# An MLP in split float32 on one Trainium2 core: when its first and last operands are formed, and when x1 is copied out

## The chip, the core and the metric

The kernel runs on one core of a Trainium2 chip. The core has five engines that work side by side and wait for each other by semaphores: TensorE (PE in the profile; PEld is its weight load), VectorE (DVE), ScalarE (ACT), GpSimd (POOL) and SyncE (SP), whose queue issues nearly all DMAs here. The metric is the device time of one execution in microseconds (us), the median of three runs. The kernel before takes 1250.95 us (1249.01 to 1251.21).

## What is computed

One decoder layer for a prompt of 1024 tokens and a sample group of 8 x 8 tokens: a mixing part (retention, window attention, two convolutions, an output projection) and then an MLP, all in float32. The change lies in the MLP, so the reference is cut to that:

```python
x = x + gate1[:, None] * mixed
h2 = rms_norm(x, norm2_g[l]) * (1.0 + scale2[:, None]) + shift2[:, None]
ff = jnp.square(jax.nn.relu(h2 @ w_ff1[l])) @ w_ff2[l]     # 1024 -> 4096 -> 1024
x = x + gate2[:, None] * ff
```

## The kernel before

Everything is held feature by feature on the 128 partitions, tokens along the free axis. `x1` (128 x 8 x 1088) is x after the first residual: 1024 prompt columns and 64 sample columns. Float32 products are made of two parts: an operand is cast to fp32r on ACT (`ah`, `qh`, `wh`: the high part), DVE subtracts that from the original (`al`, `ql`, `wl`: the low part), and a product is three matmuls, high by high, high by low, low by high. `two` (line 1260) makes both parts at once; `form` (line 1386) makes the cast and hands back the subtraction, to be placed later. A 128 x 1024 cast and the subtraction behind it are the unit of work that this text speaks of.

**First product (ff1).** The 4096 hidden features are 32 blocks of 128 rows, four blocks to a group, so 8 groups. A block is computed in three chunks of columns (384, 384 and 320, the last with the sample's 64). A chunk of a block is 24 matmuls (`ff1_block`), and ACT then applies Relu and Square into the group's tiles (`ff1_out`). `Group.quarter(i, j)` is rows 2i and 2i+1 of the group's four blocks, prompt columns 512j to 512j+511; each quarter is a tile of 128 x 1024 (`q11`, `q12`, `q21`, `q22`).

**Second product (ff2).** Group g's 512 hidden rows times w_ff2's 512 x 1024 is a 2 x 2 by 2 x 2 product of quarters. For groups 0 to 6 it is done with seven quarter products in place of eight (Strassen's scheme in Winograd's form): sums of weight quarters (`s`) and of activation quarters (`t`) are formed on DVE, split in two parts, and each of the seven `slot`s is four PE products of six matmuls each, whose results DVE adds to `x1`. Between the slots the 12 ff1 chunks of the next group are spread (`ff1_items`; f counts them, block f // 3, chunk f % 3). The sample's columns go through PE apart: `sample_parts` makes the tile `st` (a cast and a subtraction), `sample_product` multiplies it with weight parts into the bank `sm`, `sample_out` adds the result to `acc`. The last group, 7, is done with plain products, sixteen PE products of twelve matmuls each (i, t and m in line 1579 on), and closes the residual: `x1 * gate + xr + ps * gate`, where `xr` is x1 as it was before the MLP. Since DVE adds the products into `x1` itself, x1 is copied to DRAM first (`save`, line 1377) and read back in 8 pieces (line 1562).

**Order.** PE's instructions keep the order of the program throughout. ACT's and DVE's do from line 1378 on (`pinned`); ahead of it a scheduler places them. SP's DMA issues are placed by the scheduler. Each engine's queue is served in order: an instruction that waits holds up all behind it. Buffers come from pools by tag; `w`, `ar`, `wh`, `wl`, `ah`, `al`, `qh`, `ql` and `q12` have two each, `fr`, `t` and the other quarters one. A new tile of a tag waits until the readers of the tile before the last are done. `w` and `ar` take the weight quarters from DRAM, `fr` the ff1 weights of the blocks from 4 on. PE's results go round seven PSUM banks (`next_bank`).

The places of the change. (1) Ahead of the loop: blocks 0 to 3 of ff1 chunk by chunk, then the split of block 4's weights, then `first_parts` (line 1431): the sum `t`, and both parts of weight quarter (0,0) and activation quarter (0,0), which slot 1 multiplies. (2) The same `first_parts` at the end of each group (line 1544), behind slot 7 and the sample products and ahead of the last ff1 chunk, f = 11. (3) The end of the last loop turn and the sixteen plain products (lines 1547 to 1595), where all of the last group's operands are split one after another.

Of the kernel before, what the change touches and what calls it, by code (L numbers as in the profile page):

```python
# [15 lines left out]
P = 128  # L16
# [124 lines left out]
def decoder_step(ctx: ExitStack, tc: tile.TileContext, A, O, where):  # L141
# [1042 lines left out]
    with ExitStack() as fctx:  # L1184
# [54 lines left out]
        def make_h2(c):  # L1239
            c0, w = CH[c]  # L1240
            h2[c] = act_chunk(c)
            r = room("t")[:, :w]
            ps = misc_psum()[:, :w]
            average(ps, ones_r, ssq_parts[c])
            rstd(ps, w, r, ut(w))
            b = mod[:, 24:32, :]
            for k in range(8):
                modulated(h2, c, k, x1[:, k, c0 : c0 + w], r, a2, b, ut(w))
            if c == 2:
                t = sums[:, 0:512].rearrange("p (k n) -> p k n", k=8)  # L1250
                DVE.tensor_tensor(out=t, in0=x1[:, :, SEQ:], in1=r[:, PROMPT[2] :].unsqueeze(1).to_broadcast([P, 8, 64]),
                                  op=ALU.mult)
                modulated_sample(h2, t, a2, b)
# [6 lines left out]
        def two(raw, hi_tag, lo_tag):  # L1260
            hi, lo = room(hi_tag, F32R), room(lo_tag, F32R)
            cast(raw, hi, lo)()
            return hi, lo
# [33 lines left out]
        def quarter(g, i, j):  # L1297

            raw = room(RAW[turn["raw"] % 4])
            turn["raw"] += 1  # L1300
            nc.sync.dma_start(raw.rearrange("p (q f) -> p q f", q=2),
                              A["w_ff2"][g, 2 * i : 2 * i + 2].rearrange("q p f -> p q f")[:, :, H * j : H * j + H])
            return raw
# [42 lines left out]
        def ff1_load(x, tag="fr"):  # L1346
            if x < NG * G:
                ff1_weights[x] = loaded_weight(A["w_ff1"][x], room(tag))

        def ff1_split(x, hi="wh", lo="wl"):  # L1350
            if x < NG * G:
                ff1_weights[x] = two(ff1_weights[x], hi, lo)
# [4 lines left out]
        def ff1_out(u, x, c, ps):  # L1357
            for cols, dst in u.pieces(x % G, c):
                ACT.activation(dst, ps[:, cols], AF.Relu)
                ACT.activation(dst, dst, AF.Square)  # L1360


        for b in range(G):
            ff1_load(b, "w" if b < 2 else "ar")
            ff1_split(b, *(("wh", "wl") if b < 2 else ("ah", "al")))
        u = Group()
        for c in range(3):
            for b in range(G):
                ps = mm_psum(CH[c][1])
                ff1_block(u, b, c, ps)  # L1370
                if c == 0 and b == 1:
                    make_h2(2)
                ff1_out(u, b, c, ps)
        ff1_load(G)

        save = nc.dram_tensor("x1_save", (P, 8, SEQ), F32, kind="Internal").ap()
        nc.sync.dma_start(save, x1[:, :, 0:SEQ])
        pinned[0] = True
        acc = wide_room("acc")
        BANKS = [f"mm{x}" for x in range(4)] + [f"pm{x}" for x in range(3)]  # L1380
# [5 lines left out]
        def form(raw, side):  # L1386

            parts = room(side + "h", F32R), room(side + "l", F32R)
            return parts, cast(raw, *parts)
# [13 lines left out]
        def sample_parts(g, u):  # L1403

            st = up.tile([P, G, P], F32R, tag="st", name=nm("st"), bufs=1)
            ACT.copy(st[:, :, 0:64], u.sample)
            DVE.tensor_tensor(out=st[:, :, 64:P], in0=u.sample, in1=st[:, :, 0:64], op=ALU.subtract)
            return st
# [16 lines left out]
            return pp.tile([P, 512], F32, tag="pm3", name=nm("sm"))  # L1425

        sub, add = ALU.subtract, ALU.add
        ff1_split(G)
        ff1_load(G + 1)

        def first_parts(g, u, a11):

            t = room("t")
            DVE.tensor_tensor(out=t, in0=u.quarter(0, 1), in1=u.quarter(0, 0), op=sub)
            w, r0 = form(a11, "a")
            v, r1 = form(u.quarter(0, 0), "q")
            r0()
            r1()
            return t, (w, v)

        a11 = quarter(0, 0, 0)
        t, now_parts = first_parts(0, u, a11)
        s = quarter(0, 1, 0)
        a22, a12 = quarter(0, 1, 1), quarter(0, 0, 1)

        for g in range(NG - 1):
            nu = Group()
# [2 lines left out]
            def ff1_items(n):  # L1450
                for _ in range(n):
                    f = state["f"]
                    state["f"] += 1
                    b, c = f // 3, f % 3
                    x = G * (g + 1) + b
                    ps = next_bank()[:, : CH[c][1]]
                    ff1_block(nu, x, c, ps)
                    ff1_out(nu, x, c, ps)
                    if c == 0:
                        ff1_split(x + 1)  # L1460
                        ff1_load(x + 2)
# [68 lines left out]
            slot(parts6, [(1, 1, 0, 0), (0, 1, 1, 0)], [r0, r1])  # L1530
            last = g + 1 == NG - 1
            s = quarter(g + 1, 0 if last else 1, 1 if last else 0)
            ff1_items(2)


            w, r0 = form(a21, "a")
# [4 lines left out]
            sample_out(g, 1, sm)  # L1541
            if not last:
                a11 = nxt
                t, now_parts = first_parts(g + 1, nu, a11)
                a22, a12 = quarter(g + 1, 1, 1), quarter(g + 1, 0, 1)
            else:
                weights, parts = {(0, 0): two(nxt, "ah", "al")}, {(0, 0): two(nu.quarter(0, 0), "qh", "ql")}
            ff1_items(1)
            u = nu


        g = NG - 1
        weights[0, 1] = two(s, "ah", "al")
        for ij, tags in (((1, 0), ("qh", "ql")), ((0, 1), ("q12", "t")), ((1, 1), ("fr", "q11"))):
            parts[ij] = two(u.quarter(*ij), *tags)
        st = sample_parts(g, u)
        for j in range(2):
            weights[1, j] = two(quarter(g, 1, j), "wh", "wl")
        xr = [hp.tile([P, 4, CH[0][1]], F32, tag=("hi0", "lo0", "hi1", "lo1")[m % 4], name=nm("xr")) for m in range(8)]
        xr = [x.rearrange("p a b -> p (a b)")[:, 0:SEQ] for x in xr]  # L1560
        for m in range(8):
            nc.sync.dma_start(xr[m], save[:, m, :])
        s22 = x1[:, 4:8, H:SEQ]
        for x in (x1[:, 0:4, H:SEQ], x1[:, 4:8, 0:H]):
            DVE.tensor_tensor(out=x, in0=x, in1=s22, op=ALU.add)

        def sample_end(i):

# [8 lines left out]
            nc.sync.dma_start(O["yT"][:, 4 * i : 4 * i + 4, SEQ:], x)  # L1577

        for i in range(2):
            sm = sample_bank()  # L1580
            for j in range(2):
                sample_product(sm, st, weights[i, j], j, j == 0, j == 1)
            sample_out(g, i, sm)
            for t in range(2):
                for m in range(4):
                    ps = next_bank()
                    for j in range(2):
                        products(ps, m, weights[i, j], parts[j, t], j == 0, j == 1)
                    x = x1[:, 4 * i + m, H * t : H * t + H]
                    gate = mod[:, 40 + 4 * i + m, 0:1]  # L1590
                    DVE.scalar_tensor_tensor(x, x, gate, xr[4 * i + m][:, H * t : H * t + H], ALU.mult, ALU.add)
                    DVE.scalar_tensor_tensor(x, ps, gate, x, ALU.mult, ALU.add)
                    if t == 0 and m == 1:
                        sample_end(i)
                    nc.sync.dma_start(O["yT"][:, 4 * i + m, H * t : H * t + H], x)


# [72 lines left out]
```

## Time and profile before

| | |
|---|---|
| median of three runs | 1250.95 us (1249.01 to 1251.21) |
| the profiled execution, its own time | 1249.56 us |
| its span, first to last instruction | 1247.8 us |
| mean granted TensorE clock | 0.992 of full |
| PE busy | 1215.0 us (97% of the span) |
| DVE busy | 819.2 us (66%) |
| ACT busy | 469.8 us (38%) |
| DMA, HBM read and written | 101.90 MB and 10.72 MB |

The profile is one execution, taken by the hardware profiler. A line such as `ps<-qh,ah` names the tile written and the tiles read, by the program's names. Engines overlap, so shares add up to more than 100%. A matmul is shown from its start to its modelled end, and the next one starts before that end: 128 x 512 matmuls follow each other every 0.23 us though each is shown with 0.39 us. A bracket at the end of a line of the timeline, such as `[0.44 <-DVE ql L158]`, is the time for which the engine stood idle ahead of it and what ended that. Line 158 is the helper that records ACT's and DVE's instructions and line 171 the one that records PE's, so places are told apart by tile names.

### The profile page before, as it was taken

How to read it: one execution, taken by the hardware profiler on the slowest of the kernel's cores; microseconds unless marked ns; L12 is line 12 of the kernel's file. 1: busy time of each engine (PE TensorE's matmuls, PEld its weight loads, DVE VectorE, ACT ScalarE, POOL GpSimd, SP SyncE). 2: the span in 40 equal slices, each digit the busy share in tenths (PEclk: the TensorE clock that was granted, in tenths of full speed). 3: DMA queues.
4: the chain of work that ended last, by engine and by line, in shares of the span. 5: the costliest groups of instructions: out<-in, count | busy, mean ns of one | idle time of the engine just before them, and what ended most of it. 6: DMA issues, size and time to landing. Idle time of an engine off the chain costs nothing.

```text
span 1247.8 us, 17276 instructions
## 1 busy us (share of the span) xinstructions
PE 1215.0 (97%) x7044; PEld 1099.9 (88%) x7044; DVE 819.2 (66%) x1297; ACT 469.8 (38%) x943; POOL 30.0 (2%) x43
## 2 busy tenths in 40 slices
PE   8899999999999999989999999999999999999978
PEld 6797789998899999979989989989989989989967
DVE  4779798884797538546466666566475575575574
ACT  5362333342366315533333334333333333333320
POOL 3300000000000000000000000000000000000000
PEclk9899999999999999989999999999999999999989
DMA  9548811111020811311211221221121221211512
GB/s 364 180 142 306 231 52 51 50 38 35 35 71 22 279 47 34 136 34 51 74 62 68 68 56 64 68 83 53 56 79 51 68 68 51 85 51 51 185 55 89
DMA packets 54982, 113.73 MB, mean 91 GB/s; under 512 B 13431, under 2 KB 22391, under 8 KB 54903
## 3 DMA queue, kind: packets, MB, share of 16 engines
q1 hardware_dynamic: 54759, 112.56, 27.6%
q8 instruction: 55, 0.90, 0.3%
q14 instruction: 24, 0.20, 0.1%
q10 hardware_dynamic: 144, 0.07, 0.0%
HBM read 101.90 MB, written 10.72 MB: 90 GB/s over the span
## 4 chain that ended last, share of the span: by engine, by line
PE 87%; DVE 9%; DMA 2%; ACT 1%; issue 1%; SPq 0%; DVEq 0%
PE ps L171 48%; PE mm L171 29%; PE pm L171 5%; PE sm L171 3%; DVE x L158 1%; PE pm L175 1%; PE ada L171 1%; DVE al L158 1%; DVE ql L158 1%; DMA ada<-in_ada 1%; DMA M<-in_xT 1%; DMA glu<-in_st_conf 0%; ACT ah L158 0%; DVE qh L301 0%; DVE lo L308 0%
## 5 line engine op out<-in xcount | busy, mean ns | idle before, releaser
L171 PE MATMUL ps<-hi,wl 128*128 128x384 f32 (+1 forms) x672 | 219.4, 326 | 0.0
L171 PE MATMUL ps<-hi,wh 128*128 128x384 f32 (+1 forms) x672 | 219.2, 326 | 0.0
L171 PE MATMUL ps<-lo,wh 128*128 128x384 f32 (+1 forms) x672 | 219.0, 326 | 0.0
L171 PE MATMUL mm<-hi,wh 128*128 128x384 f32 (+1 forms) x536 | 178.4, 333 | 0.1
L171 PE MATMUL mm<-lo,wh 128*128 128x384 f32 (+1 forms) x536 | 174.8, 326 | 2.0 <-DVE lo L476 2.0
L171 PE MATMUL mm<-hi,wl 128*128 128x384 f32 (+1 forms) x536 | 174.4, 326 | 0.5 <-DVE wl L252 0.5
L158 ACT ACTIVATE q<-ps 128x384 f32<-128x384 f32 (+1 forms) x112 | 42.6, 381 | 350.9 <-PE ps L171 350.9
L158 DVE TENSOR_TENSOR x<-x,ps 128x512 f32<-128x512 f32 x264 | 165.9, 682 | 1.0
L171 PE MATMUL ps<-ql,ah 128*128 128x512 f32 x408 | 160.9, 394 | 4.4 <-DVE ql L158 4.4
L171 PE MATMUL ps<-qh,ah 128*128 128x512 f32 x408 | 159.9, 392 | 3.9 <-ACT qh L158 3.9
L171 PE MATMUL ps<-qh,al 128*128 128x512 f32 x408 | 160.0, 392 | 0.0
L171 PEld LDWEIGHTS ps<-hi,wh 128*128 128x128 f32 x672 | 126.2, 188 | 2.2
L171 PEld LDWEIGHTS ps<-lo,wh 128*128 128x128 f32 x672 | 126.1, 188 | 2.2
L171 PEld LDWEIGHTS ps<-hi,wl 128*128 128x128 f32 x672 | 126.1, 188 | 0.0
L158 DVE TENSOR_TENSOR wl<-fr,wh 128x1024 fp32r<-128x1024 f32 x28 | 34.3, 1225 | 134.4 <-ACT wh L158 134.4
L171 PEld LDWEIGHTS mm<-hi,wh 128*128 128x128 f32 x536 | 100.6, 188 | 7.7 <-issue 6.0
L171 PEld LDWEIGHTS mm<-lo,wh 128*128 128x128 f32 x536 | 100.7, 188 | 2.9 <-DVE lo L476 2.9
L171 PEld LDWEIGHTS mm<-hi,wl 128*128 128x128 f32 x536 | 100.6, 188 | 0.8 <-DVE wl L252 0.8
L609 DVE SCALAR_TENSOR_TENSOR M<-glu,cmix,M 128x512 f32<-128x512 f32 (+2 forms) x150 | 98.1, 670 | 2.0
L171 PEld LDWEIGHTS ps<-ql,ah 128*128 128x128 f32 x408 | 77.0, 189 | 22.1 <-DVE ql L158 7.1
L171 PEld LDWEIGHTS ps<-qh,ah 128*128 128x128 f32 x408 | 77.2, 189 | 19.0 <-ACT qh L158 4.2
L171 PEld LDWEIGHTS ps<-qh,al 128*128 128x128 f32 x408 | 77.0, 189 | 16.0
(340 smaller groups left out, 1876.9 us busy)
## 6 DMA issues: line engine op xcount, KB each, us to landing
w<-in_w_ff SPq DMA_DIRECT2D x29, 512.0 KB, 3.6
ar<-in_w_ff SPq DMA_DIRECT2D x28, 512.0 KB, 3.7
fr<-in_w_ff SPq DMA_DIRECT2D x28, 512.0 KB, 3.6
w<-in_w_in SPq DMA_DIRECT2D x22, 512.0 KB, 5.1
M<-in_ada SPq DMA_DIRECT2D x20, 512.0 KB, 4.7
ada<-in_ada SPq DMA_DIRECT2D x16, 512.0 KB, 10.4
sw<-in_ada SPq DMA_DIRECT2D x9, 512.0 KB, 5.2
w<-in_w_out SPq DMA_DIRECT2D x8, 512.0 KB, 3.6
```

The source lines that it names most:

```text
L158: i = f(*args, **kw)
L171: return tc.keep_in_program_order(nc.tensor.matmul(*args, **kw))
L175: return tc.keep_in_program_order(nc.tensor.transpose(*args, **kw))
L609: DVE.scalar_tensor_tensor(dst, src(t), cdw[:, j, t : t + 1], dst, ALU.mult, ALU.add))))
```

## The change

Seven edits.

- The last chunk of the first four blocks (c = 2) is computed in the block order 2, 3, 0, 1.
- Ahead of it the four weight quarters of group 0 are requested, and behind them x1's copy to DRAM, now in three pieces by columns. Block 4's weights are requested earlier, in chunk 0.
- The parts of slot 1's operands in group 0 are made by `two` in the buffers `ah`, `al`, `qh`, `ql` within the last chunk, and `t` behind it (`first_sum`).
- In each group one ff1 chunk, f = 10, moves from ahead of slot 7 to behind it, and the parts of the next slot 1 are made ahead of both remaining chunks, with `t` behind the parts.
- In the last loop turn the same place makes the parts of (0,0), then of weight quarter (0,1) in `wh`, `wl`, ahead of f = 10, and those of activation quarter (1,0) between f = 10 and f = 11.
- The sixteen plain products start at once. The parts of the remaining activation quarters and of the sample are made behind the first of them, the remaining weight quarters' behind the third and fourth, the sample's products come behind the fourth, its end behind the sixth.
- The two wide additions of `s22` to x1 are taken apart, one behind the first product and one ahead of the eighth's closing.

```diff
         u = Group()
+        save = nc.dram_tensor("x1_save", (P, 8, SEQ), F32, kind="Internal").ap()
         for c in range(3):
-            for b in range(G):
+            for b in range(G) if c < 2 else (2, 3, 0, 1):
                 ps = mm_psum(CH[c][1])
                 ff1_block(u, b, c, ps)
                 if c == 0 and b == 1:
                     make_h2(2)
+                    ff1_load(G)
                 ff1_out(u, b, c, ps)
-        ff1_load(G)
-
-        save = nc.dram_tensor("x1_save", (P, 8, SEQ), F32, kind="Internal").ap()
-        nc.sync.dma_start(save, x1[:, :, 0:SEQ])
+                if c == 1 and b == 3:
+                    a11 = quarter(0, 0, 0)
+                    s, a22, a12 = (quarter(0, *ij) for ij in ((1, 0), (1, 1), (0, 1)))
+                    for c0, w in zip((0, 384, 768), PROMPT):
+                        nc.sync.dma_start(save[:, :, c0 : c0 + w], x1[:, :, c0 : c0 + w])
+                if c == 2 and b == 3:
+                    now_parts = two(a11, "ah", "al"), two(u.quarter(0, 0), "qh", "ql")
+        ff1_split(G)
+        ff1_load(G + 1)
...
-        def first_parts(g, u, a11):
+        def first_sum(u):
             t = room("t")
             DVE.tensor_tensor(out=t, in0=u.quarter(0, 1), in1=u.quarter(0, 0), op=sub)
-            w, r0 = form(a11, "a")
-            v, r1 = form(u.quarter(0, 0), "q")
-            r0()
-            r1()
-            return t, (w, v)
+            return t
...
             slot(parts6, [(1, 1, 0, 0), (0, 1, 1, 0)], [r0, r1])
             last = g + 1 == NG - 1
             s = quarter(g + 1, 0 if last else 1, 1 if last else 0)
-            ff1_items(2)
+            ff1_items(1)
...
             if not last:
                 a11 = nxt
-                t, now_parts = first_parts(g + 1, nu, a11)
+                now_parts = two(a11, "ah", "al"), two(nu.quarter(0, 0), "qh", "ql")
+                t = first_sum(nu)
                 a22, a12 = quarter(g + 1, 1, 1), quarter(g + 1, 0, 1)
+                ff1_items(2)
             else:
                 weights, parts = {(0, 0): two(nxt, "ah", "al")}, {(0, 0): two(nu.quarter(0, 0), "qh", "ql")}
-            ff1_items(1)
+                weights[0, 1] = two(s, "wh", "wl")
+                ff1_items(1)
+                parts[1, 0] = two(nu.quarter(1, 0), "q12", "t")
+                ff1_items(1)
             u = nu
 
         g = NG - 1
-        weights[0, 1] = two(s, "ah", "al")
-        for ij, tags in (((1, 0), ("qh", "ql")), ((0, 1), ("q12", "t")), ((1, 1), ("fr", "q11"))):
-            parts[ij] = two(u.quarter(*ij), *tags)
-        st = sample_parts(g, u)
-        for j in range(2):
-            weights[1, j] = two(quarter(g, 1, j), "wh", "wl")
+        raw = [quarter(g, 1, j) for j in range(2)]
...
         for i in range(2):
-            sm = sample_bank()
-            for j in range(2):
-                sample_product(sm, st, weights[i, j], j, j == 0, j == 1)
-            sample_out(g, i, sm)
             for t in range(2):
                 for m in range(4):
                     ps = next_bank()
                     for j in range(2):
                         products(ps, m, weights[i, j], parts[j, t], j == 0, j == 1)
+                    if i == t == m == 0:
+                        parts[0, 1] = two(u.quarter(0, 1), "qh", "ql")
+                        parts[1, 1] = two(u.quarter(1, 1), "fr", "q11")
+                        st = sample_parts(g, u)
+                    if (t, m) == (i, 0) and i == 0 or (t, m) == (1, 3) and i == 0:
+                        x = x1[:, 0:4, H:SEQ] if m == 0 else x1[:, 4:8, 0:H]
+                        DVE.tensor_tensor(out=x, in0=x, in1=s22, op=ALU.add)
...
+                    if i == 0 and t == 0 and m >= 2:
+                        weights[1, m - 2] = two(raw[m - 2], "ah", "al") if m == 3 else two(raw[0], "wh", "wl")
+                    if t == 0 and m == 3:
+                        sm = sample_bank()
+                        for j in range(2):
+                            sample_product(sm, st, weights[i, j], j, j == 0, j == 1)
+                        sample_out(g, i, sm)
+                    if t == 1 and m == 1:
+                        sample_end(i)
```

What this does to the queues is shown at three places. First DVE, at the start of the MLP's second product; before:

```order
L158 TENSOR_TENSOR wl_5311<-fr_5306,wh_5310 128x1024
L158 TENSOR_TENSOR t_5318<-q_721_5096,q_700_4929 128x1024
L158 TENSOR_TENSOR al_5321<-w_5316,ah_5320 128x1024
L158 TENSOR_TENSOR ql_5324<-q_700_4929,qh_5323 128x1024
L158 TENSOR_TENSOR w_5328<-w_5328,ar_5330 128x1024
L158 TENSOR_TENSOR al_5336<-w_5328,ah_5335 128x1024
```

and after, where `ql_5266`, `al_5262` are the low parts of slot 1's operands, `wl_5328` that of block 4's weights, `t` the activations' sum, `w_5193` the weights' sum `s` and `al_5338` its low part:

```order
L1258 TENSOR_TENSOR ql_5266<-q_700_4929,qh_5265 128x1024
L1258 TENSOR_TENSOR al_5262<-w_5191,ah_5261 128x1024
L1258 TENSOR_TENSOR wl_5328<-fr_5014,wh_5327 128x1024
L158 TENSOR_TENSOR t_5334<-q_722_5098,q_700_4929 128x1024
L158 TENSOR_TENSOR w_5193<-w_5193,ar_5195 128x1024
L158 TENSOR_TENSOR al_5338<-w_5193,ah_5337 128x1024
```

The three low parts that stood behind or around `t` stand ahead of it; `t`, `s` and the part of `s` follow as before.

Second DVE at the end of a group (the first), behind the four additions of slot 7; before:

```order
L158 TENSOR_TENSOR acc_5309<-sm_6703,acc_5309 128x512
L158 TENSOR_TENSOR t_6713<-q_859_6157,q_853_6118 128x1024
L158 TENSOR_TENSOR al_6716<-ar_6498,ah_6715 128x1024
L158 TENSOR_TENSOR ql_6719<-q_853_6118,qh_6718 128x1024
L158 TENSOR_TENSOR ar_6603<-ar_6603,w_6723 128x1024
```

and after:

```order
L158 TENSOR_TENSOR acc_5333<-sm_6676,acc_5333 128x512
L158 TENSOR_TENSOR al_6687<-ar_6500,ah_6686 128x1024
L158 TENSOR_TENSOR ql_6691<-q_853_6120,qh_6690 128x1024
L158 TENSOR_TENSOR t_6694<-q_859_6159,q_853_6120 128x1024
L158 TENSOR_TENSOR ar_6605<-ar_6605,w_6696 128x1024
```

The parts come ahead of the sum `t`. Not to be seen on DVE: PE now has two ff1 chunks to do behind this place, where it had one.

Third ACT at the end, where `ps` in the rows are ff1 chunks f = 10 (128 and 256 columns) and f = 11 (256 and the sample's 64); before, from f = 11's first output on:

```order
L158 ACTIVATE q_1399_10078<-ps_10268 128x256
L158 ACTIVATE q_1399_10078<-q_1399_10078 128x256
L158 ACTIVATE us_9790<-ps_10268 128x64
L158 ACTIVATE us_9790<-us_9790 128x64
L158 CAST ah_10297<-ar_10156 128x1024
L158 CAST qh_10301<-q_1386_10003 128x1024
L158 CAST q_1428_10305<-q_1349_9712 128x1024
L158 CAST fr_10309<-q_1399_10078 128x1024
L158 CAST st_10313<-us_9790 128x4x64
L158 CAST wh_10318<-ar_10316 128x1024
L158 CAST wh_10324<-w_10322 128x1024
```

and after, from the cast of weight quarter (0,1) on:

```order
L158 CAST wh_10241<-ar_10158 128x1024
L158 ACTIVATE q_1386_10005<-ps_10245 128x128
L158 ACTIVATE q_1386_10005<-q_1386_10005 128x128
L158 ACTIVATE q_1399_10080<-ps_10245 128x256
L158 ACTIVATE q_1399_10080<-q_1399_10080 128x256
L158 CAST q_1425_10274<-q_1386_10005 128x1024
L158 ACTIVATE q_1399_10080<-ps_10278 128x256
L158 ACTIVATE q_1399_10080<-q_1399_10080 128x256
L158 ACTIVATE us_9792<-ps_10278 128x64
L158 ACTIVATE us_9792<-us_9792 128x64
L158 CAST qh_10340<-q_1349_9714 128x1024
L158 CAST fr_10344<-q_1399_10080 128x1024
```

Two of the seven casts that stood behind f = 11's outputs now stand ahead of them; the other five follow in the same order.

## Rows read from the trace of the kernel before

**Rows 1.** The page, part 1: busy time, share of the span, instructions.

```profile
PE 1215.0 (97%) x7044; PEld 1099.9 (88%) x7044; DVE 819.2 (66%) x1297; ACT 469.8 (38%) x943; POOL 30.0 (2%) x43
```

**Rows 2.** Waits of PE from 520 us on: us in total, times, longest.

```profile
PE sm L171 <- DVE st L158: 7.8, 4, 7.3
PE ps L171 <- DVE ql L158: 4.4, 7, 2.0
```

**Rows 3.** Timeline of PE, 544 to 552 us: start, us, engine, line, operation, tiles.

```profile
544.83 0.31 PE L171 MATMUL mm<-hi,al 128*128 128x320 f32 x1
549.03 0.79 PE L171 MATMUL ps<-qh,ah 128*128 128x512 f32 x1 [3.90 <-ACT qh L158]
551.81 0.80 PE L171 MATMUL ps<-ql,ah 128*128 128x512 f32 x1 [1.98 <-DVE ql L158]
```

**Rows 4.** Timelines of ACT, DVE and PE, 545 to 563 us.

```profile
545.92 0.24 ACT L1360 ACTIVATE us<-us 128x64 f32<-128x64 f32 x1
...
548.26 1.22 DVE L158 TENSOR_TENSOR t<-q,q 128x1024 f32<-128x1024 f32 x1
...
552.92 1.05 ACT L158 CAST ah<-w 128x1024 fp32r<-128x1024 f32 x1 [3.94 <-DVE w L158]
...
561.07 0.41 DVE L158 TENSOR_TENSOR st<-us,st 128x256 fp32r<-128x256 f32 x1
...
562.83 0.39 PE L171 MATMUL sm<-ah,st 128*128 128x512 f32 x1
```

**Rows 5.** Timelines of PE and ACT, end of the second loop turn.

```profile
732.98 0.40 PE L171 MATMUL ps<-qh,ah 128*128 128x512 f32 x1
733.82 0.50 PE L171 MATMUL ps<-ql,ah 128*128 128x512 f32 x1 [0.44 <-DVE ql L158]
...
734.16 0.26 ACT L158 ACTIVATE us<-us 128x64 f32<-128x64 f32 x1
734.93 1.05 ACT L158 CAST ah<-ar 128x1024 fp32r<-128x1024 f32 x1 [0.52 <-DVE ar L158]
...
743.64 0.47 PE L171 MATMUL sm<-ah,st 128*128 128x512 f32 x1
```

**Rows 6.** The chain that ended last, 1174 to 1197 us: start, us, what.

```profile
1174.96 5.48 PE ps L171 x24
1180.45 1.81 PE sm L171 x8
1182.26 3.53 PE ps L171 x24
...
1193.13 3.75 PE sm L171 x8
```

**Rows 7.** Timelines of ACT and PE, 1170 to 1194 us.

```profile
1170.84 0.49 ACT L158 ACTIVATE q<-ps 128x384 f32<-128x384 f32 x1 [6.53 <-PE ps L171]
...
1175.00 0.28 ACT L158 ACTIVATE q<-ps 128x128 f32<-128x128 f32 x1 [3.11 <-PE ps L171]
...
1176.25 1.03 ACT L158 CAST ah<-ar 128x1024 fp32r<-128x1024 f32 x1
...
1193.13 0.77 PE L171 MATMUL sm<-ah,st 128*128 128x512 f32 x1 [7.35 <-DVE st L158]
```

**Rows 8.** Windows: stretch, length, busy time by engine, PEclk (granted clock), DMA, GB/s.

```profile
27.00:30.00 3.00, 1.18 (x6) 0.81 (x5) 3.00 (x3) 3.00 (x6) 2.28 (x2) 1.00 1.03 411
...
48.00:51.00 3.00, 2.52 (x10) 2.23 (x11) 2.90 (x5) 0.00 (x0) 1.29 (x2) 0.81 0.00 0
...
1190.00:1195.00 5.00, 1.87 (x5) 1.52 (x6) 5.00 (x6) 3.02 (x4) 0.00 (x0) 0.50 0.01 3
```

**Rows 9.** Timeline of PE, two stops early in the program.

```profile
29.77 0.91 PE L171 MATMUL mm<-lo,wh 128*128 128x384 f32 x2 [1.82 <-DVE lo L476]
...
48.48 0.44 PE L171 MATMUL pm<-lo,wh 128*128 128x384 f32 x1 [1.96 <-DVE lo L476]
```

**Rows 10.** DMA issues: out<-in, queue, operation, count, KB each, us to landing.

```profile
x_save<-x SPq DMA_DIRECT2D x1, 4096.0 KB, 12.3
```

More of the change, by code (lines that the diff above doesn't have):

```diff
@@ L1427, in decoder_step @@
         sub, add = ALU.subtract, ALU.add
-        ff1_split(G)
-        ff1_load(G + 1)
-        def first_parts(g, u, a11):
+        def first_sum(u):
             t = room("t")
             DVE.tensor_tensor(out=t, in0=u.quarter(0, 1), in1=u.quarter(0, 0), op=sub)
-            w, r0 = form(a11, "a")
-            v, r1 = form(u.quarter(0, 0), "q")
-            r0()
-            r1()
-            return t, (w, v)
[L1441 to L1444, printed above, removed]
+            return t
+        t = first_sum(u)
         for g in range(NG - 1):
@@ L1563, in decoder_step @@
         s22 = x1[:, 4:8, H:SEQ]
-        for x in (x1[:, 0:4, H:SEQ], x1[:, 4:8, 0:H]):
-            DVE.tensor_tensor(out=x, in0=x, in1=s22, op=ALU.add)
         def sample_end(i):
@@ L1592, in decoder_step @@
                     DVE.scalar_tensor_tensor(x, ps, gate, x, ALU.mult, ALU.add)
-                    if t == 0 and m == 1:
+                    nc.sync.dma_start(O["yT"][:, 4 * i + m, H * t : H * t + H], x)
+                    if i == 0 and t == 0 and m >= 2:
[6 more added lines that the diff above has]
+                    if t == 1 and m == 1:
                         sample_end(i)
-                    nc.sync.dma_start(O["yT"][:, 4 * i + m, H * t : H * t + H], x)
 def kernel(**inputs):
```

## The prediction, made before the changed kernel had run

> **What bounds the kernel now.** Read the page's first part first: PE is busy for 97% of the span [rows 1]. No other engine is near, so a change that removes no matmul can only take PE's stops away, together with the slow clock behind them. The second view is therefore the list of PE's waits over the MLP [rows 2]: 7.8 us for `st`, 7.3 of it in one piece, and 4.4 us for `ql` in seven pieces; a 3.90 us wait for `qh` comes on top [rows 3]. The third view is the timeline at these stops. They lie at three kinds of place. At the start of the second product PE's last ff1 matmul starts at 544.83, slot 1's first at 549.03 and its second at 551.81 [rows 3]. At each group's end slot 1's second matmul starts 0.84 us behind its first instead of 0.23 [rows 5]. At the end PE stands for 7.35 us ahead of the sample product [rows 7]. All have one cause: operands are split while PE has nothing else to do.
>
> The unit prices: a cast takes 1.03 to 1.05 us on ACT, a wide sum or subtraction 1.22 on DVE [rows 4, 5]. A slot is 24 matmuls, 5.45 us without the overlap of its last one; the sample's eight matmuls are 1.81, a chunk of 320 columns 3.53 [rows 6]. A chunk of 384 columns is 4.16, the distance of two chunks' outputs, 1170.84 and 1175.00 [rows 7].
>
> **The start.** Removed: both stops, since slot 1's four parts are now made during the last chunk's four blocks (4 x 3.53 = 14 us). The rows of the order bear that out: `ql`, `al` and block 4's `wl` stand ahead of `t`. Block order 2, 3, 0, 1 frees the first `ah`, `al` with its first block, and quarter (0,0) is complete since chunk 1. So slot 1 starts with the last block's end, 544.83 + 0.15 = 545.0, in place of 549.03. Not removed: the chain to slot 2 and to `st`. `t` reads quarter (0,1), and the new block order finishes just that quarter last. The last Square ends at 545.92 + 0.24 = 546.2 [rows 4]; `t` to 547.4, the weight sum to 548.6; then the cast of the sum. From that cast to the sample product the DVE queue holds one low part, two copies into x1, another low part, six copies and `st`. Between the cast's start and the sample product that takes 743.64 - 734.93 = 8.7 us at a group's end [rows 5], and 8.6 to the end of `st` here, from 552.92 to 561.07 + 0.41 [rows 4]. So the sample product starts at 548.6 + 8.7 = 557.3, against 562.83 before: **5.5 us gained**. PE arrives there at 545.0 + 5.45 + 4.16 = 554.6, so a new stop of 2.7 us appears, some 2.4 to 2.5 in the profile's way of counting.
>
> That new stop can cost more than itself. After a stop shown as 1.82 us at 29.77 the next stretch shows the full granted clock; after one of 1.96 us at 48.48 the clock fell, to a mean of 0.81 over 48 to 51 us [rows 8, 9]. At the lower level, 1.2 GHz, the sample's eight matmuls at the end took 3.75 us where eight at the upper one took 1.81 [rows 6], about 1.7 us lost once the overlap of the last is left out. My stop is longer than the one that was followed by a fall, so I take **1.7 us lost**, with 0 as the other end. By the Trainium skill, TensorE: Matmul & The Clock Gate, section HAM oscillation — how this bites in real kernels, waits between bursts of matmuls slow the clock, and half of the time spent slow is lost. By that rule the loss here would be the same; without a fall the sum ends 1.7 us lower. The trace agrees with the half: 3.75 against 1.81.
>
> **The group ends, six that lead to a slot 1.** The parts now stand ahead of `t` on DVE and have two ff1 chunks (4.16 + 3.53 = 7.7 us) of cover, where they had one. Two casts, `acc` and two subtractions need about 4.5, so the stop on `ql` (0.6 us start to start) goes. What is late next is `st` again. In the rows, slot 1 starts at 732.98, PE would reach the sample product at 732.98 + 5.45 + 4.16 = 742.6 and starts it at 743.64; its chain begins with the cast at 734.93, which stood 0.52 us waiting for the weight sum [rows 5]. With `t` and that sum done during f = 10 and f = 11, this wait goes, but the cast can't start ahead of f = 11's last output (734.16 + 0.26, same engine, ahead in the queue). So the sample product comes 0.5 us earlier, and a stop of some 0.5 stays. Six times 0.5: **3.0 us gained**. The bounds are 0 (the sum is still late) and 1.0 each, all that PE loses at such a place.
>
> f = 10 leaves slot 7 one chunk less ahead of it: its parts have f = 9 alone, 4.16 us. They were made in slot 6, their casts over 6 us ahead of f = 9's output, as ACT's idle of 6.53 shows [rows 7], so nothing is late. The cast of slot 7's last weight quarter (1176.25, right behind f = 10's output) now follows f = 9's; its low part is needed 5.45 + 0.9 us later. On SP the weight quarters' requests keep their order and come no later.
>
> **The end.** In the frame of before: slot 7 starts 4.16 earlier, at 1170.8; the sample products end at 1178.1; f = 10 runs to 1182.3, f = 11 to 1185.8, where it ends today. The first plain product can follow if its parts are there. (0,0)'s and weight (0,1)'s: three casts and three subtractions behind `acc`, done by 1182.3. Activation (1,0)'s: f = 10's output takes ACT 1.25 us (1175.00 to 1176.25), then the cast 1.03, then `t` 1.22: 1182.4 + 3.5 = 1185.9, needed from 1185.8 + 6 x 0.23 = 1187.2. The cover is 1.3 us, and each us beyond it would cost one. Behind it: the other quarters and `st` by 1191, needed at 1196.7 (four products of 2.72); the second row of weights by about 1201.4, behind one wide addition and the closing pairs of 1.5 us, needed at 1210. The second half of `xr` now waits for f = 10's end, 1182.3; four pieces of 512 KB take some 6 us by the price of x1's copy [rows 10], and DVE wants the first about 1196. So the stop of 7.35 us goes (7.5 start to start), and the slow clock behind it, 0.50 granted from 1190 to 1195 [rows 8], with 1.7: **9.2 us gained**. The products behind it and the last DMA are as many as before.
>
> **x1's copy.** It was issued when x1's last columns were done and landed 12.3 us later [rows 10], long before DVE first overwrites x1. It now goes in three pieces, the last of them a quarter of it, behind the four weight quarters. Cost nothing: DVE's first copy would come about 551 (548.6 plus a cast and a low part).
>
> **Sum.** 5.5 - 1.7 + 3.0 + 9.2 = 16.0 us. The profiled execution took 1249.56 us, so 1233.6; it lies 1.4 us below the median of its runs, so a median may come out up to 1235. I take 1234, and 1232 to 1236 as the likeliest case's own range.
>
> **Rivals.** (1) No fall of the clock at the new stop: for it, 29.77's stop had none; against it, mine is longer than 48.48's. Time: 1249.56 - 17.7 = 1231.9, with the median's offset up to 1233.3.
> (2) A new wait at the end takes a part back: the low part of activation (1,0), 1.3 us of cover, or DVE's work during the first plain products holding the second weights. For it: DVE has 15 us of queue there without a pause. Against: 6 to 9 us of cover for all but the first. Price 2 to 4 us: 1235.5 to 1238.
> (3) The change doesn't do what it says at the group ends and the start: `st` alone sets the pace, so the group ends give 0 and the start 3. Against: the 0.52 us wait of the cast is in the row [rows 5]. Time: 1249.56 - 3 + 1.7 - 9.2 = 1239, to 1241.
> (4) Also `st` gets ahead of PE at the group ends, 1.0 each: 1230.6, or 1229 without a fall of the clock. Against: the chain of 8.7 us behind f = 11's output has no gap.
> (5) Slower than before: x1's copy. DVE's first copy into x1 has to wait for its last piece, and DVE's queue holds `st` and every later part, so PE stops one us for each us of delay. It decides from 551 on; the 16 us are used up when the last piece lands at 567, and 570 is slower by over 0.2%. For it: pieces and quarters share one queue, and the rows get shorter. Against: 4096 KB took 12.3 us [rows 10]; the request stands ahead of the last chunk's four blocks, so ahead of 531, and to land at 570 a quarter of those bytes would need 39 us. Price at 575: 1257.
>
> **How the numbers follow.** Forecast 0.50, rival 1 0.27, rival 2 0.10, rival 3 0.05, rival 4 0.03, rival 5 0.03, and 0.02 for a run with no gain at all. The range 1230.5 to 1238 holds the forecast, rival 1 and most of rival 2, some 0.85. About 0.2%, 2.5 us, is what a measurement of this kernel can tell from no change: faster by more 0.95, within 0.02, slower 0.03.
>
> **What would show it.** After: no wait for `qh` or `ql` at the first slot 1, and `sm` waiting for `st` about 2.4 us near 555 us; a granted clock of 0.5 for a few us behind it (rival 1: full). At six group ends no wait on `ql`, and the first `sm` waiting 0.3 to 0.5 for `st`. At the end the first plain product right behind f = 11, no stop over 0.3, and granted clock full throughout. A wait of PE on `t` or `xr`-held banks there would show rival 2; a DVE copy waiting for `x_save`, rival 5. Wrong in the sum if the stop at 555 is much longer than 2.7 us: then the chain from Square to `st` was read wrongly.

## The result

| | before | after |
|---|---|---|
| median | 1250.01 us (1249.01 to 1251.21, 4 runs) | 1232.07 us (1231.87 to 1234.55, 4 runs) |
| ratio after to before, 95% interval | | 0.9857 (0.9842 to 0.9872) |
| span of the profiled execution | 1247.8 us | 1230.3 us |
| mean granted TensorE clock | 0.992 | 0.996 |

The change makes the kernel 1.4% faster: 17.9 us of the median, 17.5 us of the span. The forecast was 1234 us, from a sum of 16.0 us gained.

The page of the kernel after, its first part, and the list of PE's waits from 520 us to the end (in all, times, longest):

```profile
PE 1210.6 (98%) x7044; PEld 1099.0 (89%) x7044; DVE 818.1 (66%) x1297; ACT 468.7 (38%) x943; POOL 30.1 (2%) x43
```

```profile
PE sm L171 <- DVE st L158: 3.5, 7, 2.3
```

The waits for `qh` and `ql` and the 7.3 us piece for `st` [rows 2] are gone. Seven waits for `st` are left, one of 2.3 us at the start and six small ones at the group ends. (A wait as listed is some 0.16 us shorter than the distance of the starts shows: 0.21 listed is 0.37 from start to start.) The start on PE's timeline, the kernel after:

```profile
543.99 0.31 PE L171 MATMUL mm<-hi,wl 128*128 128x320 f32 x1
544.13 0.39 PE L171 MATMUL ps<-qh,ah 128*128 128x512 f32 x1
...
553.62 0.34 PE L171 MATMUL ps<-hi,wl 128*128 128x384 f32 x1
556.21 0.50 PE L171 MATMUL sm<-ah,st 128*128 128x512 f32 x1 [2.26 <-DVE st L158]
...
560.15 0.52 PE L171 MATMUL ps<-lo,wh 128*128 128x384 f32 x1
560.47 0.52 PE L171 MATMUL ps<-hi,wl 128*128 128x384 f32 x1
...
561.06 0.34 PE L171 MATMUL ps<-lo,wh 128*128 128x384 f32 x1
561.24 0.34 PE L171 MATMUL ps<-hi,wl 128*128 128x384 f32 x1
```

Slot 1 starts 0.14 us behind ff1's last matmul, where it was 4.20 [rows 3]. The first sample product now has the stop, 2.26 us as listed. Some 1.4 us behind it matmuls of 384 columns follow each other every 0.32 us, up to 561.06, in place of 0.17: the lower clock. The granted clock by stretch (us, PE's busy time, clock, DMA share, GB/s) has it too; it is still full ahead of 557 us and 0.50 from 557.6 on:

```profile
555.00:560.00 5.00, 3.79 (x14) 0.76 0.30 88
560.00:565.00 5.00, 5.00 (x25) 0.90 0.36 122
```

```profile
553.00:557.00 4.00, 1.74 (x9) 1.00 0.00 0
557.60:561.00 3.40, 3.40 (x12) 0.50 0.70 210
```

DVE's queue between slot 1's start and `st`, the kernel after:

```profile
545.20 1.23 DVE L158 TENSOR_TENSOR t<-q,q 128x1024 f32<-128x1024 f32 x1 [2.23 <-ACT q L1360]
546.35 1.22 DVE L158 TENSOR_TENSOR w<-w,ar 128x1024 f32<-128x1024 f32 x1
548.68 1.23 DVE L158 TENSOR_TENSOR al<-w,ah 128x1024 fp32r<-128x1024 f32 x1 [1.12 <-ACT ah L158]
549.83 1.28 DVE L158 COPY x<-ps 128x512 f32<-128x512 f32 x2
551.03 1.21 DVE L158 TENSOR_TENSOR ql<-t,qh 128x1024 fp32r<-128x1024 f32 x1
552.16 3.67 DVE L158 COPY x<-ps 128x512 f32<-128x512 f32 x6
555.75 0.41 DVE L158 TENSOR_TENSOR st<-us,st 128x256 fp32r<-128x256 f32 x1
```

`t` waits for the last Square of quarter (0,1), as the prediction read from the block order. The chain runs on without a pause but the cast's. DVE's first copy into x1, at 549.83, has no wait: x1's copy to DRAM had landed at 506.2.

At a group's end, the place of [rows 5], ACT's cast now follows the last output at once (ACT's timeline, kernel after), and PE's stop is 0.21 us as listed (PE's timeline):

```profile
728.80 0.26 ACT L158 ACTIVATE us<-us 128x64 f32<-128x64 f32 x1
728.96 1.03 ACT L158 CAST ah<-ar 128x1024 fp32r<-128x1024 f32 x1
```

```profile
737.65 0.47 PE L171 MATMUL sm<-ah,st 128*128 128x512 f32 x1 [0.21 <-DVE st L158]
```

At the end, the place of [rows 7], PE goes from f = 11's last matmul straight into the plain products, and the sample product behind the fourth of them waits for nothing:

```profile
1177.10 0.31 PE L171 MATMUL ps<-hi,wl 128*128 128x320 f32 x1
1177.25 0.39 PE L171 MATMUL ps<-qh,ah 128*128 128x512 f32 x1
...
1188.16 0.39 PE L171 MATMUL sm<-ah,st 128*128 128x512 f32 x1
```

The clock of the last stretch, 0.50 before [rows 8], is full:

```profile
1190.00:1195.00 5.00, 5.00 (x24) 1.00 0.27 102
```

**The sum, measured.** Both traces are cut at ff1's last matmul ahead of the second product: 544.83 in before, 543.99 in after. From there to the end of the span the kernel before takes 702.97 us and the one after 686.31, so 16.66 us are gained, against 16.0 forecast. By places, in starts of PE's matmuls:

- to the first sample product 18.00 us before and 12.22 after: 5.78 gained;
- from it to slot 4's sample product 36.90 and 38.58: 1.68 lost;
- six group ends: 3.45 gained (below);
- from the first sample product of the last loop turn (group 6) to the end 142.05 and 132.94: 9.11 gained.

The other 0.84 us of the span lie ahead of 490 us, in code that is the same in both: one and the same matmul of PE starts at 489.59 in before and at 488.74 in after, and from it to ff1's last matmul both take 55.2 us.

### The profile page after: what moved, and what is told of

Same layout as the page of the kernel before. It is cut to its first block, busy times and chain, and to the rows that moved or that the text cites. A ratio compares the mean times of both kernels' runs of the same rounds, so it can differ in the third digit from the quotient of the medians.

```text
span 1230.3 us, 17273 instructions
## 1 busy us (share of the span) xinstructions
PE 1210.6 (98%) x7044; PEld 1099.0 (89%) x7044; DVE 818.1 (66%) x1297; ACT 468.7 (38%) x943; POOL 30.1 (2%) x43
## 4 chain that ended last, share of the span: by engine, by line
PE 87%; DVE 9%; ACT 2%; DMA 1%; issue 1%; SPq 0%; DVEq 0%
PE ps L171 48%; PE mm L171 29%; PE pm L171 5%; DVE x L158 3%; PE sm L171 3%; PE pm L175 1%; PE ada L171 1%; DMA ada<-in_ada 1%; DVE al L158 1%; DMA M<-in_xT 1%; DVE ql L158 1%; ACT ah L158 1%; ACT q L158 0%; DVE qh L301 0%; DVE lo L308 0%
## 5 line engine op out<-in xcount | busy, mean ns | idle before, releaser
L158 ACT ACTIVATE q<-ps 128x384 f32<-128x384 f32 (+1 forms) x112 | 42.5, 380 | 353.3 <-PE ps L171 353.3
L158 DVE TENSOR_TENSOR x<-x,ps 128x512 f32<-128x512 f32 x264 | 165.1, 679 | 0.4 <-PE ps L171 0.4
L158 DVE TENSOR_TENSOR wl<-fr,wh 128x1024 fp32r<-128x1024 f32 x27 | 33.1, 1225 | 101.8 <-ACT wh L158 101.8
```

The lines of the kernel that those rows point to most:

```text
L158: i = f(*args, **kw)
```

## Experiments

The table holds what all of them gave. "Stretch" is the time from ff1's last matmul ahead of the second product to the end of the span, in the profiled execution. Nearly every edit acts in it (from 490 us to its start all thirteen profiled executions take 55.23 to 55.26 us), so it tells more than the time of the whole, as the section on what was unexpected shows. Before is 702.97 us, after 686.31.

| kernel | median, us | ratio to before (95%) | stretch, us | to before |
|---|---|---|---|---|
| e_start | 1246.76 | 0.9971 (0.9961 to 0.9982) | 698.75 | -4.22 |
| e_groups | 1247.60 | 0.9976 (0.9965 to 0.9987) | 701.07 | -1.90 |
| e_chunk | 1247.50 | 0.9968 (0.9957 to 0.9980) | 699.32 | -3.65 |
| e_order | 1252.76 | 1.0014 (1.0004 to 1.0024) | 705.10 | +2.13 |
| e_end | 1241.34 | 0.9928 (0.9914 to 0.9943) | 694.35 | -8.62 |
| e_copy | 1232.18 | 0.9855 (0.9840 to 0.9870) | 686.19 | -16.78 |
| e_after2 | 1234.08 | 0.9869 (0.9853 to 0.9885) | 686.39 | -16.58 |
| e_sample | 1235.74 | 0.9877 (0.9861 to 0.9894) | 688.84 | -14.13 |
| e_blocks | 1229.64 | 0.9833 (0.9818 to 0.9847) | 682.55 | -20.42 |
| e_st | 1227.21 | 0.9810 (0.9795 to 0.9824) | 679.60 | -23.37 |
| e_both | 1226.84 | 0.9816 (0.9800 to 0.9831) | 679.72 | -23.25 |

**The start alone** (`e_start`: the kernel before with the edits ahead of the loop, and the old group ends and end).

```diff
-            for b in range(G):
+            for b in range(G) if c < 2 else (2, 3, 0, 1):
...
+                if c == 2 and b == 3:
+                    now_parts = two(a11, "ah", "al"), two(u.quarter(0, 0), "qh", "ql")
...
-        t, now_parts = first_parts(0, u, a11)
+        t = first_sum(u)
```

> Only the start's edits (block order 2, 3, 0, 1 in the last chunk, slot 1's parts and block 4's split made within it, x1's copy in three pieces); the group ends and the end are those of the kernel before. Theory A (operands formed sooner; st's chain then sets the pace): 5.5 to 5.8 us gained up to the first sample product, 1.5 to 1.7 given back by the slow clock behind the stop of 2.4, so about 4 us faster than before, 1246. Rival B (only PE's two stops count, 3.9 and 2.0 with the slow clock, and st isn't late): 8 us faster, 1242. Rival C (x1's copy in pieces collides with the weight quarters): no gain or slower.

Measured: 1246.76 us. On PE's timeline the first sample product comes 12.23 us behind ff1's last matmul and slot 4's 38.57 us behind it, as in after (12.22 and 38.58). The stop and the slow clock behind it belong to these edits, and the net gain of the place is 5.77 - 1.67 = 4.1 us.

**The group ends alone, whole and in halves** (`e_groups`: chunk f = 10 moved and the parts put ahead of `t`; `e_order`: only the parts ahead of `t`; `e_chunk`: only the chunk moved).

```diff
-            ff1_items(2)
+            ff1_items(2 if last else 1)
...
-                t, now_parts = first_parts(g + 1, nu, a11)
+                now_parts = two(a11, "ah", "al"), two(nu.quarter(0, 0), "qh", "ql")
+                t = first_sum(nu)
...
-            ff1_items(1)
+            ff1_items(1 if last else 2)
```

`e_order` has the middle piece alone, `e_chunk` the first and the last.

> Only the six group ends: parts ahead of the sum t, and f = 10 moved behind slot 7; start and end as before. Theory A: the wait on ql goes, the wait on st grows to 0.4 start to start, 0.6 gained at five places and 0.4 at one, 3.4 us in all, 1246.6. Rival B (all that PE loses there goes): 5.5 to 6 us. Rival C (st alone sets the pace): within 0.5 us of before.

> Half of the group ends' edit: the parts are made ahead of t on DVE, but f = 10 stays ahead of slot 7, so they have one chunk of cover. Theory A (the sum that the cast waits for still ends at the same time, so st's chain does too): PE's wait on ql goes and comes back at st, 0 to 0.5 us gained in all. Rival B (the order of parts and t makes the gain): about 3 us, as with the chunk moved.

> The kernel before with only the chunk f = 10 moved behind slot 7's products (six group ends); the first parts keep their old order behind t. Theory A (the second chunk is the cover, the order behind it does not matter, since al, ql, t and the weight sum are all done within two chunks): no wait for ql, the distance of the group ends' sample products falls from 90.52 to 89.9 us, 3 to 3.4 us in all, about 1247.5. Rival B (chunk and order only work together): with t ahead, ql is still late, the distance stays within 0.2 us of 90.52, and the time is that of the kernel before, about 1250.5.

Measured, as the distance from one group's first sample product to the next one's, mean of five: before 90.53 us, `e_groups` 89.93, `e_chunk` 89.93, `e_order` 90.52. The first place gains 0.44 (53.39 to 52.95) in the first two as well. So the chunk alone brings all of the 3.4 us, and the order of parts and `t` brings nothing: rival B of `e_chunk` falls. PE's waits for `st` and `ql` from 520 us on, in `e_order` and in `e_chunk`:

```profile
PE sm L171 <- DVE st L158: 12.8, 7, 7.3
...
PE ps L171 <- DVE ql L158: 2.5, 2, 2.3
```

```profile
PE sm L171 <- DVE st L158: 8.6, 7, 7.3
...
PE ps L171 <- DVE ql L158: 2.0, 1, 2.0
```

In `e_order` five of the waits for `ql` went, and the time came back in the next wait: the sample product's stop is 1.00 us, where the two stops of before were 0.61 and 0.30 (start to start, at five places). At the first group end it lost 1.12 us, which I had not expected. In before `t` runs there while DVE waits for the first cast; in `e_order` DVE stands idle for that time, and `t` and the weight sum behind it end 1.1 us later, measured from that cast. DVE's first low part in before and in `e_order`:

```profile
640.88 1.23 DVE L158 TENSOR_TENSOR al<-ar,ah 128x1024 fp32r<-128x1024 f32 x1 [1.56 <-ACT ah L158]
```

```profile
644.29 1.23 DVE L158 TENSOR_TENSOR al<-ar,ah 128x1024 fp32r<-128x1024 f32 x1 [2.69 <-ACT ah L158]
```

So the cast behind the weight sum waits longer (ACT's timeline, `e_order`; the same row of before has `[0.35 <-DVE w L158]`):

```profile
648.95 1.05 ACT L158 CAST ah<-w 128x1024 fp32r<-128x1024 f32 x1 [1.48 <-DVE w L158]
```

The rest of `e_order`'s 2.13 us, 1.05, lies ahead of the first sample product, in code that it doesn't change. The stop there is the same (3.89 us, then slot 1's second matmul 2.77 us behind its first), but the clock fell at another point. In before it is 0.50 at slot 1's first matmul; in `e_order` it is still full there, and more matmuls run slowly behind it, up to 559.46 in place of 554.96 (us, PE's busy time, clock, DMA share, GB/s; before, then `e_order`):

```profile
549.03:555.05 6.02, 4.04 (x9) 0.50 0.45 119
```

```profile
551.40:552.78 1.38, 0.50 (x1) 1.00 0.77 107
552.78:559.60 6.82, 5.43 (x13) 0.50 0.40 133
```

`e_groups` shows the same, 1.03 us, and 0.50 more behind the stop at the end; that is why its stretch gained 1.90 and not 3.4.

**The end alone** (`e_end`: the last loop turn and the plain products of the kernel after; start and group ends of before).

```diff
+                weights[0, 1] = two(s, "wh", "wl")
+                ff1_items(1)
+                parts[1, 0] = two(nu.quarter(1, 0), "q12", "t")
+                ff1_items(1)
...
-            sm = sample_bank()
-            for j in range(2):
-                sample_product(sm, st, weights[i, j], j, j == 0, j == 1)
-            sample_out(g, i, sm)
```

> Only the end: the last loop turn's chunk order, the plain products' operands made in the new order and buffers, the sample's products behind the fourth product. Theory A: the stop of 7.5 us start to start and the slow clock behind it go, 9.1 us faster, about 1241, and PE has no stop over 0.3 us from the last slot 7 on. Rival: a new wait at the first plain product for the low part of activation quarter (1,0), 6 us or less gained.

Measured: 1241.34 us, and from the first sample product of the last loop turn to the end 132.83 us against 142.05, so 9.22 gained. Start, group ends and end, each alone, give 4.1, 3.4 and 9.2 at their own places, together 16.7: the parts add up. Their whole stretches give less, 4.22 + 1.90 + 8.62 = 14.74: `e_end`, too, lost 0.60 at the start that it shares with before, by where the slow clock fell.

**The sample ahead of the plain products** (`e_sample`: the kernel after with `st` and the first sample products where they were).

```diff
+        st = sample_parts(g, u)
         for i in range(2):
+            if i == 0:
+                sm = sample_bank()
+                for j in range(2):
+                    sample_product(sm, st, weights[i, j], j, j == 0, j == 1)
+                sample_out(g, i, sm)
```

> The changed kernel with the sample's parts made first and its products ahead of the first plain product, where before had them; the other operands' places are kept. Theory A: PE waits for the sample's tile, whose last Square comes 1.2 us behind f = 11 and is followed by a cast of 0.4 and a subtraction of 0.4: a stop of 2.2 to 2.6 us and perhaps a slow clock (up to 1.7), so 2.2 to 4.3 us slower than the changed kernel, 1234 to 1236; so of the end's 9.1 us some 5 to 7 come from the parts made ahead of f = 11's outputs and the rest from the sample's place. Rival (the sample's place is the whole gain): 9 us slower.

Measured: the last stage takes 135.48 us, 2.54 more than in after, nearly all of it one stop (2.47 from start to start), with the full clock behind it:

```profile
1179.06 0.31 PE L171 MATMUL ps<-hi,wl 128*128 128x320 f32 x1
1181.68 0.47 PE L171 MATMUL sm<-ah,st 128*128 128x512 f32 x1 [2.31 <-DVE st L158]
```

So of the 7.5 us that PE stood ahead of the sample product, parts made a chunk or two sooner take 5 away, and the sample's move behind four products the last 2.5. The sample's move on top of the kernel before, without the sooner parts, was not run.

**x1's copy** (`e_copy`: the kernel after with the copy in one piece, behind the last chunk).

```diff
-                    for c0, w in zip((0, 384, 768), PROMPT):
-                        nc.sync.dma_start(save[:, :, c0 : c0 + w], x1[:, :, c0 : c0 + w])
...
+        nc.sync.dma_start(save, x1[:, :, 0:SEQ])
```

> The changed kernel with x1's copy to DRAM in one piece and requested behind the last chunk, as the program of before has it. Theory A (the copy has 40 us of cover either way): within 0.5 us of the changed kernel, 1232. Rival (the copy's place is part of the gain at the start, since DVE's first copies into x1 wait for it): 2 us slower or more.

Measured: 1232.18 us and a stretch of 686.19 us against 686.31. The pieces do not matter here. The edit moved the request less than the program shows: `e_copy` issues the whole copy at 501.4, after its last piece at 501.5, and they land at 513.7 and 506.2, over 35 us ahead of DVE's first copy into x1. The weights' requests that the change puts sooner in the program moved as little: block 4's goes out at 415.7 in before and at 414.9 in after, the last weight quarter's at 491.2 and 490.4. The DMA rows of after (KB each, us to landing):

```profile
x_save<-x SPq DMA_DIRECT2D x2, 1536.0 KB, 6.0
x_save<-x SPq DMA_DIRECT2D x1, 1024.0 KB, 4.7
```

**What is left, and a version that beats both.** `e_blocks` is after with the last chunk's blocks in the order 2, 0, 1, 3, so that quarter (0,1) is complete one block sooner. `e_st` is after with `st`'s low part on DVE (`st_low`) ahead of the last four copies into x1 in slot 1. `e_both` has both. `e_after2` is the kernel after once more.

```diff
-            for b in range(G) if c < 2 else (2, 3, 0, 1):
+            for b in range(G) if c < 2 else (2, 0, 1, 3):
...
-                if c == 2 and b == 3:
+                if c == 2 and b == 0:
                     now_parts = two(a11, "ah", "al"), two(u.quarter(0, 0), "qh", "ql")
...
-            slot(now_parts, [(0, 0, 0, 1), (1, 1, 0, 1)], [r0, r1])
-            st = sample_parts(g, u)
+            slot(now_parts, [(0, 0, 0, 1), (1, 1, 0, 1)], [r0, r1, st_low])
```

> The changed kernel with the last chunk's block order 2, 0, 1, 3 instead of 2, 3, 0, 1 and slot 1's parts placed accordingly: quarter (0,1) is complete one block (3.5 us) sooner. Theory A (the stop near 556 us hangs on the last Square of that quarter): t and the weight sum come 3.5 us sooner, the cast of the sum about 2 to 3, the stop of 2.4 us and the slow clock behind it (1.65) go; up to 0.5 may be lost at slot 1's second product, whose bank the last block used: 3.5 to 4 us faster than the changed kernel, about 1228.3. Rival (the stop hangs on the wait for weights from DRAM): no change.

> The changed kernel with one more edit: in slot 1 the low part of st is placed on DVE behind the third product's turn, ahead of the last four additions instead of behind all eight. Theory A (what is left is the length of DVE's queue from the weight sum's cast to st): the chain is shorter by 4 x 0.6 = 2.4 us, so the six stops of 0.45 go (2.7 us) and the one at the start (2.4 us) all but goes, and with it the slow clock (1.65): 6.5 us faster than the changed kernel, about 1225.5. Rival (st's cast on ACT or the sample's tile is late, not DVE's queue): no gain.

> The changed kernel with both last edits of the experiments: the last chunk's blocks in the order 2, 0, 1, 3 and st's low part third in slot 1's row on DVE. Theory A (PE's stops for st are all that is left behind 545 us, and either edit alone takes the first of them): no stop of PE over 0.2 us from 545 us to the end, 679 to 680 us from slot 1's first matmul to the end as with st's low part moved alone, so 1225 to 1228, no better than that. Rival B (the two gain on different things and add): 1223 to 1225.

> The changed kernel once more, unaltered, beside the two others. Both theories: 1230 to 1234; from slot 1's first matmul to the end 686 us as before within 1 us, and what differs lies ahead of 545 us, in code that no kernel here changes.

Measured: `e_after2` has the stretch of after (686.39), though its median is 2.0 us higher and just over the 1234 expected. `e_blocks` takes 3.76 us off the stretch, by the missing stop and slow clock at the start; its group ends stay. `e_st` takes off 6.71: 3.95 at the start, 2.67 at the group ends. `e_both` is equal to `e_st` (679.72 and 679.60): the two take the same stop at the start. In `e_st` PE has no listed wait left, and the row of the stretch reads (PE's busy time in 655 us, granted clock):

```profile
545.00:1200.00 655.00, 655.00 (x3440) 1.00 0.22 71
```

That is the answer to what bounds it then: PE's own matmuls at the full clock. At 1227.21 and 1226.84 us the two are 1.9% and 1.8% faster than the kernel before by the ratios of the table, and 5 us faster than the kernel after (1232.07). The cause that the prediction named, `st` behind DVE's six copies, is shown by it: DVE's rows of `e_st` have `st` ahead of four of the copies, and PE doesn't wait.

```profile
554.67 1.29 DVE L158 COPY x<-ps 128x512 f32<-128x512 f32 x2
555.87 0.42 DVE L158 TENSOR_TENSOR st<-us,st 128x256 fp32r<-128x256 f32 x1
556.20 2.48 DVE L158 COPY x<-ps 128x512 f32<-128x512 f32 x4
```

## Why the prediction was right

- **The start, 5.5 gained: 5.78 measured** (5.77 in `e_start`). The chain was read rightly: it starts with the quarter's last Square (the prediction took the end of the sample's, some 0.15 us later), and from the cast (547.60) to the sample product (556.21) it took 8.61 us where I had 8.7 from [rows 4, 5]. The new stop was forecast at 2.4 to 2.5 as listed, and is 2.26. That the gain is so near is in part luck: the 18.00 us of before are one execution's, and the other four profiled kernels with that start took 17.88 to 19.06, by where the slow clock fell, so the gain is 5.7 to 6.8 us.
- **The slow clock, 1.7 lost: 1.68 measured**, and the same within 0.02 in `e_start`, `e_sample`, `e_copy` and `e_after2`, which all have this stop. By the Trainium skill, TensorE: Matmul & The Clock Gate, section HAM oscillation — how this bites in real kernels, half of the time spent slow is lost. The trace agrees: the matmuls are at the slow distance from about 557.6 to 561.06, 3.5 us, and 1.68 are lost. So the size was right, but to 0.02 by luck: it was carried over from the end of before, where the clock was already at 0.50 when PE went on and 3.5 us of slow matmuls followed (the rows below, from before), while here it was still full at the sample product and fell 1.4 us behind it. The prediction had no ground for the two slow stretches to be equally long; at the start of before and of `e_order` they were not. The reason that I gave for the fall, that this stop is longer than one of 1.96 us, is not borne out: see the last section. Rival 1 (no fall) did not occur here.

```profile
1189.00:1193.00 4.00, 0.00 (x0) 0.62 0.00 0
1193.20:1196.70 3.50, 3.50 (x9) 0.50 0.02 5
```

- **The group ends, 3.0: 3.45 measured.** The direction and the place were right; the term was sized a little low, 0.60 at five places and 0.44 at the first in place of 0.5. What I put down to two things, the order ahead of `t` and the moved chunk, is the chunk's alone (`e_chunk`, `e_order`). The stop left on `st` was forecast at 0.3 to 0.5 and is listed as 0.21.
- **The end, 9.2: 9.11 measured** (9.22 in `e_end`). The narrowest cover, the low part of activation (1,0), was forecast at 1.3 us. DVE ends it at 1176.24 + 1.23 = 1177.47, and it is wanted from 1177.25 + 6 x 0.23 = 1178.6: 1.2 us. Rival 2 named this place; the cover held, and no wait came.
- **x1's copy, 0: 0 measured**, by DVE's first copy without a wait and by `e_copy`. Rival 5 was out of reach.
- **Against the sum.** 16.66 of the 17.5 us of span are the terms; the 0.84 that remain lie ahead of 490 us, in code that the change leaves alone, and were no part of the forecast.

## What to carry over

When one engine is busy for 97% of the span, look for the few places where its operands are made with nothing else queued on it, and move independent work of that engine, here one ff1 chunk, into the gap; at the group ends, moving the preparing instructions past each other on their own engine gained nothing and at one place cost 1.1 us. A low part that many microseconds of queue separate from its cast is better put ahead of work that nobody waits for yet: one DVE subtraction of 0.42 us, moved ahead of four copies or additions at seven places, was worth 6.7 us. For edits of a few microseconds compare the stretch that they touch, cut at the same instruction in both traces, beside the time of the whole.

## What was unexpected

The same code ends at different times in different executions: ff1's last matmul starts at 543.8 to 547.2 us in the profiled ones, and all of that spread is there at 490 us, ahead of the first matmul that an edit touches. The granted clock goes with it. The first 60 us and the stretch from 300 to 360 us, in after and in `e_order` (us, PE's busy time, clock, DMA share, GB/s):

```profile
0.00:60.00 60.00, 51.11 (x336) 0.94 0.75 276
...
300.00:360.00 60.00, 59.39 (x545) 1.00 0.15 46
```

```profile
0.00:60.00 60.00, 50.50 (x312) 0.91 0.75 276
...
300.00:360.00 60.00, 59.74 (x535) 0.97 0.14 43
```

After's last ff1 matmul starts at 543.99, `e_order`'s at 547.20. Executions with 0.94 and 1.00 came at 543.8 to 544.8 (before, after, `e_copy`), those with one of the two lower at 545.0 to 546.1 (`e_blocks`, `e_chunk`, `e_end`, `e_start`, `e_groups`, `e_sample`, `e_after2`), those with both lower at 546.5 to 547.2 (`e_st`, `e_both`, `e_order`). So of the 6.7 us by which `e_st` is ahead of after in the stretch, the spans of the profiled executions show 4.2: `e_st`'s came to that point 2.5 us later. That the medians, 4.9 us apart, differ from the stretch for the same reason is likely, not shown. PE's list of waits has none over 0.4 us from 300 to 360 us, in after as in `e_order`; why an execution takes the one or the other clock stays open.

A stop's length does not settle whether the clock falls. Before's stop of 1.82 us at 29.77 was followed by the full clock [rows 9]; the row that the prediction cites for it, 27 to 30 us [rows 8], lies for the most part ahead of the stop's end, but the stretch behind it is full too. In `e_order` the stop at the same instruction, 1.84 us at 30.02, was followed by 0.63. The stretch behind it in before, then `e_order`'s stop and its stretch:

```profile
30.00:32.00 2.00, 1.98 (x11) 1.00 1.01 404
```

```profile
30.02 0.44 PE L171 MATMUL mm<-lo,wh 128*128 128x384 f32 x1 [1.84 <-DVE lo L476]
```

```profile
30.00:32.00 2.00, 0.44 (x1) 0.63 1.04 414
```

The two differ in more than this stop: `e_order` had stood for 1.25 us at 26.16, where before stood 0.52, and stood again for 2.20 us right behind it. In `e_sample` one execution has both cases: the 2.25 us stop at 558.18 was followed by the fall and the 2.31 us stop at 1181.68 was not:

```profile
560.00:565.00 5.00, 5.00 (x23) 0.70 0.64 210
```

```profile
1180.00:1185.00 5.00, 3.32 (x15) 1.00 0.14 55
```

At the start all five executions with that stop had the fall, so the term of 1.7 us held each time; the reason stated for it does not carry it. What decides the fall stays open.
